# Side work in steps twice as large, one every 1.8 dense units, with groups of prompt attention in turn and selected rows staged in DRAM

## The chip, the cores and the metric

One Trainium2 chip, one of its cores. The metric is device time of one execution in microseconds (us); lower is better. The core has TensorE (PE, with its weight loads as a row of their own, PEld), VectorE (DVE), ScalarE (ACT), GpSimd (POOL) and SyncE (SP). Here SP does nothing but issue DMAs, one after the other, and it stops at each whose semaphores have not come yet.

## The reference, cut to what matters

One layer of a hybrid decoder, for 512 prompt tokens and 8 samples of 4 new tokens each (544 columns together):

```
h = rmsnorm(x); z = h @ w_in                        # 2048 x 14376
A = sparse attention(q, k, v, gates) * silu(.)      # compressed + selected + window
B = causal pooling, group map * silu(.)
C = conv, chunked state-space scan (SSD), silu gate, rmsnorm
y = x + w_out(sum_b sigmoid(G_b) * (m_b @ w_branch_b))
```

For a sample, attention reads a paged cache, `cache_kv` (16 pages of 128 positions, found through `page_table`; a row holds k_cmp, v_cmp, k_slc and v_slc for 2 heads, 256 numbers each), and a window of 512 rows. With 33 blocks the top 16 are selected by a mask, so that the selected branch reads all rows of its pages too.

## The kernel before, in words

**Dense units.** The projections are cut into 612 `Unit`s in one fixed list: `w_in` (kv, gd, q: 84 units; nz, mz: 64; mg first half: 96; pool and xbc: 112; mg second half: 96), then `w_branch`, then `w_out`. A unit is 24 matmuls of 128x128 weights by 272 columns in fp32r: 4 slices of k, three products each (`hhi*wh`, `hlo*wh`, `hhi*wl`), two column halves, summed in a PSUM tile `zin`. Its weights come as `wr` (512 KB for two units, four buffers, L423), are issued six units ahead, and are split three units ahead by ACT (`wh`, L173) and DVE (`wl`, L176).

**Side work.** All the rest (norms, rope, attention, pooling, convolution, SSD) is written as generators. `run_units` calls `step` between dense units, and each step runs every generator in `s.sides` up to its next `yield`. `s.rate` is the number of steps per unit: 1.0, 1.5 in the first half of mg, 1.7 in the second. The order in the program is then changed by a scheduler at build time: each engine gets one fixed order, in which side instructions may stand inside a unit.

**Pools.** `U` gives one of 32 SBUF buffers of 128x608, `A` one of four PSUM banks for side work (`zin` has its own).

**Sample attention** (`samp`): for two pairs of samples, `samp_cmp` makes the compressed keys (`keys4` turns four blocks of `kr` rows through PE into `kT`; then the scores `cS` with weights of only 32 columns) and the compressed values (`pv`, `xvT`, `ocT`); then `samp_group` runs four times over window and selected rows (`kT`, scores `sS`, turned probabilities `sP`, values `sO`). `need` loads row sets two ahead of their use.

**Where the rows come from.** `stage_pages` copies the k_cmp and v_cmp half of every page to a DRAM scratch `ckd`, 128 DMAs, one per step. `rows` reads these sets from `ckd`, four DMAs of 256 KB each. Selected rows come straight from the cache instead: eight DMAs of 128 KB for one set, and for each SP must first load the page number into a register (`page`, L350):

```
if kind > 1:
    nc.sync.dma_start(u[:, o:o + 256], s.page(t, 4 * bl + e)[:, 256 * kind:256 * kind + 256])
```

**Prompt attention** (`attn_p`): for each of two groups of four heads, eight blocks a head: `sa` (scores and exp), `sb` (turn to `PT`), `sc` (values into `O`), one block a step. Both groups run as soon as their q is ready, so that they are interleaved.

Of the kernel before, what the change touches and what calls it, by code (L numbers as in the profile page):

```python
# [19 lines left out]
NP = 512  # L20
# [9 lines left out]
RATE_SSD = 1.7  # L30
RATE_MG = 1.5
# [92 lines left out]
class Prog:  # L124
    def __init__(s, ctx, tc, a):
        s.ctx, s.tc, s.nc = ctx, tc, tc.nc
        s.a = a
        s.n = 0
        s.sides = []
# [223 lines left out]
    def stage_pages(s):  # L353

        nx = s.ids(0, 1, 0, 16)
        for b in range(8):
            t, nx = nx, s.ids(b + 1, 1, 0, 16) if b < 7 else None
            for i in range(16):
                s.nc.sync.dma_start(s.ckd[b][i], s.page(t, i)[:, :512])
                yield  # L360

    def rows(s, raw, q, bl, kind, lq, t):

        nc = s.nc
        b = 2 * q + bl
        for e in range(4):
            if e % 2 == 0:
                u = s.U("kr")
                if kind < 2:
                    src = s.ckd[b].rearrange("i (c l) x -> (i c) l x", l=16)  # L370
                    nc.sync.dma_start(u[:, :512].rearrange("p (l x) -> p l x", l=2),
                                      src[:, 4 * lq + e:4 * lq + e + 2, 256 * kind:256 * kind + 256])
            o = 256 * (e % 2)
            if kind > 1:
                nc.sync.dma_start(u[:, o:o + 256], s.page(t, 4 * bl + e)[:, 256 * kind:256 * kind + 256])
            raw[bl, e] = (u, o)
# [20 lines left out]
    def run_units(s, units, ld=6, lp=3):  # L397
        n = len(units)
        acc = 0.0
        for i in range(n):  # L400
# [4 lines left out]
            if i >= 0:  # L405
                units[i].mm()
                acc += s.rate
# [57 lines left out]
    def norm_rope(s, raws, acc, gains, todo):  # L465
# [5 lines left out]
        for n, u in raws:  # L471
# [14 lines left out]
            yield  # L486

    def stage_kv(s):
# [4 lines left out]
        s.kv_done = False  # L493
        s.ksT = s.dp.tile([128, 2, 2, 32], F, name="ksT")
# [88 lines left out]
    def kv_side(s, kacc):  # L583
# [16 lines left out]
        for i in range(5):  # L600
            r0, rows = (i * 128, 128) if i < 4 else (NP, 32)
            for kind in range(3):
# [12 lines left out]
                yield  # L615
# [65 lines left out]
    def q_side(s, g, qacc):  # L681
# [8 lines left out]
        yield from s.norm_rope(raws, qacc.pop(g), {e: s.gain[:, 0:1] for e in range(4)}, todo)  # L690


    def attn_p(s, g):
        nc = s.nc
        while not s.kv_done:
# [37 lines left out]
        for e in range(4):  # L733
            h = g * 4 + e
            O = s.A("O")
            s.mm(O[:, :NP], s.vc4[32 * e:32 * e + 32, g], pc[32 * e:32 * e + 32, :NP], True, False,
                 skip_group_check=True)
            us = [(br, i) for i in range(4) for br in range(2)]
            PP, PT = {}, {}

            def sa(n):
                br, i = us[n]
                L = i * 128 + 128
                S = s.A("S")
                s.mm(S[:, :L], q[e][:, i * 128:L], s.kv[4 + 4 * br + g][:, :L], True, False)
                s.mm(S[:, L - 128:L], s.identb, s.trib, False, True)
                mx, sm = s.small(1), s.small(1)
                nc.vector.tensor_reduce(mx, S[:, :L], axis=AX.X, op=OP.max)
                s.ts(mx, mx, -1e29, OP.max, -SC, OP.mult)
                P = s.U("P")  # L750
                s.act(P[:, :L], S[:, :L], AF.Exp, bias=mx, scale=SC, accum_out=sm)
                s.ts(sm, sm, 1e-30, OP.max)
                nc.vector.reciprocal(sm, sm)
                c = h * 3 + 1 + br
                s.ts(P[:, :L], P[:, :L], sm, OP.mult, s.gn[:, i, c:c + 1], OP.mult)
                PP[n] = P

            def sb(n):
                br, i = us[n]
                P = PP.pop(n)  # L760
                L = i * 128 + 128
                t = s.A("PT")
                for kt in range(i + 1):
                    s.tr(t[:, kt * 128:kt * 128 + 128], P[:, kt * 128:kt * 128 + 128])
                PT[n] = s.U("PT")
                if n % 2:
                    s.act(PT[n][:, :L], t[:, :L])
                else:
                    nc.vector.tensor_copy(PT[n][:, :L], t[:, :L])

            def sc(n):
                br, i = us[n]
                pt = PT.pop(n)
                for kt in range(i + 1):
                    s.mm(O[:, i * 128:i * 128 + 128], s.Vn[kt][:, br * 256 + g * 128:br * 256 + g * 128 + 128],
                         pt[:, kt * 128:kt * 128 + 128], False, br == 1 and kt == i, skip_group_check=True)
            for n in range(10):
                if n < 8:
                    sa(n)
                if 1 <= n < 9:  # L780
                    sb(n - 1)
                if n >= 2:
                    sc(n - 2)
                yield
            o = s.U("Os")
            s.act(o[:, :NP], O)
            nc.sync.dma_start(s.oT[h][:, :NP], o[:, :NP])
# [3 lines left out]
        for br in range(2):  # L791
            del s.kv[4 + 4 * br + g]

# [17 lines left out]
    def pool_units(s):  # L811
# [11 lines left out]
        def u_side(t, u):  # L823
# [24 lines left out]
            for e in range(gi + 1):  # L848
# [8 lines left out]
                yield  # L857
# [124 lines left out]
    def dt_side(s):  # L982
# [12 lines left out]
        x, e, q, d = s.dtx, s.U("e"), s.U("sq"), s.U("sd")  # L995
        x, e, q, d = (v[:16, :T] for v in (x, e, q, d))
# [71 lines left out]
    def ssd(s):  # L1068
# [5 lines left out]
        for c in range(4):  # L1074
            cs = slice(c * 128, c * 128 + 128)
            xd, yo = [], []
            for g in range(2):
# [6 lines left out]
                yield  # L1084
# [8 lines left out]
            yield  # L1093
            if c:
                for g in range(2):
                    p = s.A("yo")
                    s.mm(p, CT[g][:, cs], St[g][:, :NP])
                    u = s.U("yo")
                    s.tt(s.h64(u[:, :NP]), s.h64(p), s.hb(s.eac[:, c, g * 8:g * 8 + 8]))
                    yo.append(u)  # L1100
                    yield
# [34 lines left out]
            for k in range(6):  # L1136
                if k < 4:
                    ld(k)
                if 1 <= k < 5:
                    dec(k - 1)  # L1140
                if k >= 2:
                    out(k - 2)
                yield
            for g in range(2):
# [8 lines left out]
                yield  # L1153
        osp = a["o_ssm_p"].rearrange("o b h p n -> (o b h p) n")
        for g in range(2):
# [7 lines left out]
            yield  # L1163
        yield from s.ssd_sample(BT, CT, one)
        yield from s.m_norm()
        yield from s.br_early()

    def ssd_sample(s, BT, CT, one):
# [5 lines left out]
        for g in range(2):  # L1174
# [8 lines left out]
            yield  # L1183
# [23 lines left out]
        for b in range(8):  # L1207
            load(b + 2)
            bm = s.dp.tile([32, 256], F, name=s.nm("bm"), tag="bm", bufs=2)
            s.ts(bm, nb[:32, :256], s.c("smask")[:32, b:b + 1])  # L1210
            sT = []
            for g in range(2):
# [9 lines left out]
                yield  # L1222
            for q in range(4):
                o = b * 64 + (q // 2) * 32
                s.mm(py[32 * q:32 * q + 32, :256], cz[:, o:o + 32], sT[q // 2][:, (q % 2) * 256:(q % 2) * 256 + 256],
                     b == 0, b == 7, skip_group_check=True)
            for g in range(2):
# [9 lines left out]
                yield  # L1237
# [30 lines left out]
    def m_norm(s):  # L1268
# [3 lines left out]
        for g in range(2):  # L1272
            P = [s.A("ms") for _ in range(2)]
            for e in range(4):
# [5 lines left out]
                yield  # L1280
                for hf in range(2):
                    s.mm(P[hf][:, :H], s.c("ones"), z[:, hf * H:hf * H + H], e == 0, e == 3)
            ss, rs, tmp = s.U("mss"), s.U("mrs"), s.U("mt")
# [12 lines left out]
    def samp(s):  # L1296
# [11 lines left out]
        ready, pts = [], []  # L1308

        def need(n=1):  # L1310
            while todo and len(ready) < AHEAD + n:
                q, kind, lq = todo.pop(0)
                raw = {}
                t = pts.pop(0) if pts else None
                if todo and todo[0][1] > 1:
                    pts.append(s.ids(2 * todo[0][0], 2, 4 * todo[0][2], 4))
                for bl in range(2):
                    s.rows(raw, q, bl, kind, lq, t)
# [34 lines left out]
    def keys4(s, raw, CI, out):  # L1353

        for ci, bl, g in CI:
# [10 lines left out]
            if ci % 2:  # L1366
                yield


    def samp_cmp(s, x, imp, CI, need):  # L1370
# [8 lines left out]
        for j in range(4):  # L1379
            wt = []  # L1380
            for h in range(2):
                w = W.pop(4 * h + j)
# [11 lines left out]
            yield  # L1394
            for e2 in range(2):
                p = s.A("qw")
                for e in range(2):
                    for h in range(2):
                        o = (e * 2 + h) * 128
                        c = (2 * e2 + e) * 128  # L1400
                        s.mm(p[:, o:o + 128].rearrange("p (b w) -> p b w", b=8), wt[h][:, c:c + 128], qv)
                o = QW[2 * j + e2][:, :NP].rearrange("p (e b h w) -> p e h b w", e=2, b=8, h=2)
                v = p.rearrange("p (e h b w) -> p e h b w", e=2, h=2, b=8)
                for e in range(2):
                    if e2:
                        s.act(o[:, e], v[:, e])
                    else:
                        nc.vector.tensor_copy(o[:, e], v[:, e])
            yield
        for y in range(2):  # L1410
            q = 2 * x + y
            S = s.A("cS")
            for lq in range(4):
                kT = []
# [507 lines left out]
```

## Time and profile before

| | |
|---|---|
| median of 3 runs | 2454.61 us (2452.2 to 2456.29) |
| the profiled execution's own time | 2455.51 us |
| its span in the trace | 2453.7 us |
| PE busy | 2381.8 us, 97% |
| DVE, ACT busy | 1084.9 us, 716.9 us |
| mean granted clock of PE | 0.991 |

The span is the time from the first to the last instruction; 1.8 us of the execution lie outside it. Matmuls overlap in the pipeline, so 97% is the share of time in which at least one is under way; it doesn't say that PE runs at its peak.

### The profile page before, as it was taken

To read this page: it belongs to the slowest core of one execution; us is meant where nothing else is said; L and a number is where in the kernel's file an instruction comes from. 1 tells how busy PE (TensorE), PEld (TensorE's weight loads), DVE (VectorE), ACT (ScalarE), POOL (GpSimd) and SP (SyncE) were. 2 spreads that over 40 slices of the span, in tenths; PEclk is the share of its full clock that TensorE was granted. 3 is DMA by queue.
4 is the path that set the end of the run, shared out by engine and by line. 5 is a ranking of instruction groups with operands and counts; after the bars stand their busy time and mean duration, and the time that the engine had idled before them with its cause. 6 is when DMAs were issued, how large, how long until landed. Compare 5 with 4: busy or idle time off the path is not lost. (4 is left out here: it accounts for less than half of the span.)

```text
span 2453.7 us, 49120 instructions
## 1 busy us (share of the span) xinstructions
PE 2381.8 (97%) x19749; PEld 2239.6 (91%) x19749; DVE 1084.9 (44%) x2206; ACT 716.9 (29%) x1369; POOL 55.7 (2%) x153
## 2 busy tenths in 40 slices
PE   4999999999999999999899999999999999999999
PEld 4999888888998998988798999989999999999999
DVE  5227547555332232423353545555446344445222
ACT  4222333333332222322232233322223322223221
POOL 0001011000000000000000000000000000000000
PEclk9999899999999999999999999999999999999999
DMA  7855563422568567665656543333646664443442
GB/s 213 243 160 147 168 173 99 136 69 75 154 202 246 159 192 227 174 196 162 208 160 196 143 126 89 102 105 111 183 128 196 183 189 132 133 133 99 127 132 81
DMA packets 525668, 377.27 MB, mean 154 GB/s; under 512 B 26895, under 2 KB 472615, under 8 KB 525440
## 3 DMA queue, kind: packets, MB, share of 16 engines
q1 hardware_dynamic: 518528, 360.76, 51.5%
q10 hardware_dynamic: 6912, 13.37, 1.5%
q8 instruction: 155, 2.54, 0.4%
q14 instruction: 73, 0.60, 0.1%
HBM read 328.31 MB, written 79.66 MB: 166 GB/s over the span
## 5 line engine op out<-in xcount | busy, mean ns | idle before, releaser
L153 PE MATMUL zin<-hhi,wh 128*128 128x272 f32 (+1 forms) x3616 | 784.6, 297 | 5.6 <-ACT wh L173 4.6
L176 DVE TENSOR_TENSOR wl<-wr,wh 128x512 fp32r<-128x512 f32 (+1 forms) x612 | 422.9, 693 | 776.4 <-ACT wh L173 772.9
L153 PE MATMUL zin<-hlo,wh 128*128 128x272 f32 (+1 forms) x3616 | 757.7, 290 | 0.0
L153 PE MATMUL zin<-hhi,wl 128*128 128x272 f32 (+1 forms) x3616 | 756.5, 290 | 0.2 <-DVE wl L176 0.2
L173 ACT ACTIVATE wh<-wr 128x512 fp32r<-128x512 f32 (+1 forms) x612 | 382.9, 628 | 1108.7 <-PE zin L153 919.5
L153 PEld LDWEIGHTS zin<-hhi,wh 128*128 128x128 f32 (+1 forms) x3616 | 568.3, 189 | 38.6 <-issue 28.3
L153 PEld LDWEIGHTS zin<-hhi,wl 128*128 128x128 f32 (+1 forms) x3616 | 570.2, 189 | 4.5 <-issue 3.0
L153 PEld LDWEIGHTS zin<-hlo,wh 128*128 128x128 f32 (+1 forms) x3616 | 567.8, 189 | 6.1 <-issue 5.2
L153 PE MATMUL zin<-bh,wh 128*128 128x272 f32 x1280 | 266.4, 290 | 1.1 <-DVE gt L185 1.1
L153 PE MATMUL zin<-bl,wh 128*128 128x272 f32 x1280 | 264.7, 288 | 0.0
L153 PE MATMUL zin<-bh,wl 128*128 128x272 f32 x1280 | 264.4, 288 | 0.0
L153 PEld LDWEIGHTS zin<-bh,wh 128*128 128x128 f32 x1280 | 200.0, 188 | 1.4 <-ACT wh L173 1.3
L153 PEld LDWEIGHTS zin<-bl,wh 128*128 128x128 f32 x1280 | 201.3, 189 | 0.0
L153 PEld LDWEIGHTS zin<-bh,wl 128*128 128x128 f32 x1280 | 201.1, 188 | 0.0
L1364 DVE COPY kT<-kT 128x512 f32<-128x512 f32 x72 | 49.0, 688 | 63.7 <-PE kT L156 63.1
L156 PE MATMUL kT<-cst,kr 128*128 128x128 f32 x512 | 68.9, 276 | 0.0
L156 PEld LDWEIGHTS kT<-cst,kr 128*128 128x128 f32 x512 | 56.6, 141 | 7.7 <-issue 5.7
L173 ACT ACTIVATE mg<-zin 128x544 f32<-128x544 f32 x48 | 29.8, 620 | 101.9 <-PE zin L153 101.9
L173 ACT ACTIVATE P<-S,sm 128x512 f32<-128x512 f32 (+3 forms) x64 | 33.8, 528 | 86.6 <-DVE sm L182 84.3
L173 ACT ACTIVATE kT<-kT 128x512 f32<-128x512 f32 x72 | 42.5, 595 | 33.8 <-PE kT L156 33.2
L153 PE MATMUL S<-kv,q 128*128 128x128 f32 (+3 forms) x128 | 47.1, 452 | 0.2
L153 PE MATMUL O<-PT,Vn 128*128 128x128 f32 x320 | 44.4, 277 | 0.0
(409 smaller groups left out, 1839.4 us busy)
## 6 DMA issues: line engine op xcount, KB each, us to landing
wr<-in_w_in_dram SPq DMA_DIRECT2D x224, 512.0 KB
ckd<-in_cache_kv_dram SPq DMA_DIRECT2D x128, 256.0 KB
kr<-ckd SPq DMA_DIRECT2D x128, 256.0 KB
kr<-in_cache_kv_dram SPq DMA_DIRECT2D x256, 128.0 KB
wr<-in_w_branch_dram SPq DMA_DIRECT2D x48, 512.0 KB
wr<-in_w_out_dram SPq DMA_DIRECT2D x32, 512.0 KB
mgd<-mg ACTq DMA_DIRECT2D x48, 272.0 KB
gt<-mgd SPq DMA_DIRECT2D x48, 272.0 KB
```

The costliest lines, as they stand in the source:

```text
L153: return s.nc.tensor.matmul(out, l, r, start=start, stop=stop, **kw)
L156: return s.nc.tensor.transpose(out, in_, s.c("ident")[:k, :k])
L173: return s.nc.scalar.activation(out, in_, f, **kw)
L176: return (eng or s.nc.vector).tensor_tensor(out, a, b, op=op)
L1364: s.nc.vector.tensor_copy(u[:, :NP], p)
```

## The change

Each generator's step is made about twice as large and its stages are put one step apart, so that what a step uses on PE was made in the step before: in `samp_cmp` and `samp_group`, `scores` of set n-1 stands ahead of `keys4` of set n in one step; values take two sets a step; the probabilities of the compressed branch become a generator of their own. In return there is a step only every 1.8 units (`RATE = 0.55`, and `0.75` in the second half of mg). `attn_p` of group 1 waits until group 0 is through (`s.turn`) and does two blocks of each stage a step. `stage_pages` copies both halves of each page, 256 DMAs, and is driven once per unit by a new list `s.feeds`, whatever the rate is. Selected rows are then read from `ckd` like the others, four DMAs of 256 KB a set with addresses known at build time.

```
-RATE_SSD = 1.7
-RATE_MG = 1.5
+RATE = 0.55
+RATE_SSD = 0.75
...
-        s.rate = 1.0
+        s.rate = RATE
...
-        s.ckd = [dt(f"ckd{b}", [16, 128, 512]) for b in range(8)]
+        s.ckd = [[dt(f"ckd{k}{b}", [16, 128, 512]) for b in range(8)] for k in range(2)]
...
+        for k in range(2):
+            for b in range(8):
+                t, nx = nx, s.ids((b + 1) % 8, 1, 0, 16)
+                for i in range(16):
+                    s.nc.sync.dma_start(s.ckd[k][b][i], s.page(t, i)[:, 512 * k:512 * k + 512])
+                    yield
...
+        k, o = divmod(kind, 2)
+        src = s.ckd[k][b]
+        for e in (0, 2):
+            u = s.U("kr")
+            if k:
+                v = src[4 * lq + e:4 * lq + e + 2].rearrange("i t x -> t i x")
...
+            s.nc.sync.dma_start(u[:, :512].rearrange("p (l x) -> p l x", l=2), v[:, :, 256 * o:256 * o + 256])
+            raw[bl, e], raw[bl, e + 1] = (u, 0), (u, 256)
...
                 units[i].mm()
+                s.feeds = [g for g in s.feeds if next(g, s) is not s]
                 acc += s.rate
...
-        while not s.kv_done:
+        while not s.kv_done or s.turn != g:
             yield
...
+        for n in range(0, 36, 2):
+            for f, d in ((sc, 4), (sb, 2), (sa, 0)):
+                for m in (n - d, n - d + 1):
+                    if 0 <= m < 32:
+                        f(m)
             yield
...
+        for n in range(9):
+            if n:
+                scores(n - 1, kT)
+                kT = None
+            if n < 8:
+                kT = s.keys4(need(), CI)
+            yield
...
-            if j + 2 < 8:
-                W[j + 2] = s.cmp_w(1, j + 2)
+            if j + 3 < 8:
+                W[j + 3] = s.cmp_w(1, j + 3)
...
+        for n in range(0, 6, 2):
+            if n == 2:
+                po = begin(0, nt)
+            if n:
+                for m in (n - 2, n - 1):
+                    sums(po, P.pop(m), need(), 0, m == 3)
+            if n < 4:
+                for m in (n, n + 1):
+                    P[m] = turn(S[m], m)
...
-        s.sides.append(s.stage_pages())
+        s.feeds.append(s.stage_pages())
...
-        units.append(Mark(lambda: s.pace(RATE_MG)))
         units += s.mg_units(0, MGA)
-        units.append(Mark(lambda: s.pace(1.0)))
```

Two places in the built order show what moves. The first is SP's queue in the selected phase of the second sample group. Before, this is the end of a run of selected rows (`pt` is a page table row, `TENSOR_LOAD` and `ISA` set registers), up to the next weight load:

```order
L345 DMA pt_13795<-in_page_table_dram 1x2x4
L350 TENSOR_LOAD pt_13658
L350 ISA x2
L375 ISA
L375 DMA kr_13797<-in_cache_kv_dram 128x256
...
L350 TENSOR_LOAD pt_13658
L350 ISA x2
L375 ISA
L375 DMA kr_13860<-in_cache_kv_dram 128x256
L423 DMA wr_13888<-in_w_in_dram 128x8x128
```

Now, a set of selected rows stands between two weight loads (`no` are small outputs of the pooling branch):

```order
L423 DMA wr_16819<-in_w_in_dram 128x8x128
L374 DMA kr_16571<-ckd_89 128x2x256
L374 DMA kr_16573<-ckd_89 128x2x256
L374 DMA kr_16575<-ckd_90 128x2x256
L374 DMA kr_16577<-ckd_90 128x2x256
L846 DMA out_dram<-no_16614 15x128
L847 DMA out_dram<-no_16614 8x4x128
L423 DMA wr_16898<-in_w_in_dram 128x8x128
```

The register loads are gone from this stretch, a set is four DMAs in place of eight, and fewer of them stand between two weight loads. In the whole program SP has 384 register loads from memory before and 256 now, 1,295 DMAs before and 1,272 now; 71 of the 256 staging copies stand behind the first load of staged rows, none of 128 before.

The second place is PE in the compressed keys of the first pair, with `cS` the scores with narrow weights and `kT` the turned keys. Before:

```order
L153 MATMUL zin_8414<-hlo,wh_8410 128x272 x2
L156 MATMUL kT_8578<-cst,kr_8119 128x128 x2
...
L156 MATMUL kT_8585<-cst,kr_8121 128x128 x2
L153 MATMUL cS_8521<-kT_8535,QW_8103 32x128
L153 MATMUL cS_8521<-kT_8542,QW_8103 32x128
L156 MATMUL kT_8620<-cst,kr_8123 128x128 x2
L153 MATMUL cS_8521<-kT_8583,QW_8103 32x128
L156 MATMUL kT_8620<-cst,kr_8125 128x128 x2
L156 MATMUL kT_8627<-cst,kr_8123 128x128
L153 MATMUL cS_8521<-kT_8590,QW_8103 32x128
```

Now the 16 scores of one set stand together, and behind them the 16 transposes of the next:

```order
L153 MATMUL zin_9937<-hlo,wh_9762 128x272 x2
L153 MATMUL cS_9974<-kT_9867,QW_9342 32x128
L153 MATMUL cS_9974<-kT_9874,QW_9342 32x128
...
L153 MATMUL cS_9974<-kT_9888,QW_9343 32x128
L156 MATMUL kT_9999<-cst,kr_9362 128x128 x2
L156 MATMUL kT_9999<-cst,kr_9364 128x128 x2
...
L156 MATMUL kT_10020<-cst,kr_9368 128x128 x2
L153 MATMUL zin_9937<-hhi,wh_9802 128x272 x2
```

The scores are no longer broken up by transposes. PE's instructions are the same 18,036 matmuls in both programs. The stretches of side work between dense matmuls fall from 425 to 285. Of stretches with 32-column weights that PE enters from 128-column work, those of `cS`, `sS`, `sO` and `nT` fall from 72 to 40. The last `O` comes 164 units into the list, before 136; the last `soT` (the end of sample attention) 333, before 315; the last `ms` (the end of the SSD branch) 403, before 417.

## Rows read from the trace of the kernel before

**Rows 1.** Busy time by stretch (from:to, length, busy; PEclk granted; DMA share, GB/s).
```profile
core 0: us, PE busy (x) PEld busy (x) DVE busy (x) ACT busy (x) POOL busy (x), PEclk, DMA share, GB/s
0.00:45.00 45.00, 13.63 (x61) 11.20 (x62) 26.32 (x74) 22.35 (x59) 0.98 (x6) 0.92 0.71 207
...
200.00:350.00 150.00, 146.46 (x1380) 131.81 (x1378) 94.29 (x161) 44.66 (x82) 18.51 (x22) 0.95 0.58 165
...
620.00:985.00 365.00, 360.18 (x3364) 336.12 (x3363) 113.66 (x212) 102.63 (x189) 1.03 (x12) 1.00 0.68 198
985.00:1430.00 445.00, 421.16 (x3677) 386.24 (x3676) 180.46 (x376) 131.50 (x271) 15.92 (x52) 0.98 0.61 176
```
**Rows 2.** The chain, in order of time: a long dense stretch (start, us).
```profile
1969.98 292.13 PE zin L153 x2328
```
**Rows 3.** Waits, 985 to 1430: us in total, times, longest.
```profile
ACT wh L173 <- DMA wr<-in_w_in_dram: 73.1, 16, 12.8
...
PE sS L153 <- ACT kT L173: 5.8, 2, 5.1
...
PE zin L153 <- ACT wh L173: 4.6, 1, 4.6
```
**Rows 4.** Timeline of SP, 1044 to 1099: start, us, instruction, count.
```profile
1046.39 1.02 SPq L423 DMA_DIRECT2D wr<-in_w_in_dram  x2
...
1055.44 8.48 SPq L375 DMA_DIRECT2D kr<-in_cache_kv_dram  x8
...
1090.20 0.43 SPq L423 DMA_DIRECT2D wr<-in_w_in_dram  x1
```
**Rows 5.** Waits, 1086 to 1098.
```profile
ACT wh L173 <- DMA wr<-in_w_in_dram: 6.0, 1, 6.0
...
PE sS L153 <- ACT kT L173: 5.1, 1, 5.1
```
**Rows 6.** Waits, 959 to 970.
```profile
PE ocT L153 <- DMA cw<-in_cmp_w_dram: 4.2, 2, 3.4
```
**Rows 7.** Waits of PE, 200 to 350.
```profile
PE dn L156 <- DVE dtx L185: 1.8, 1, 1.8
```
**Rows 8.** Busy time by stretch, columns as in rows 1, just behind that wait.
```profile
256.50:270.20 13.70, 13.70 (x89) 10.89 (x89) 3.77 (x16) 3.45 (x10) 0.00 (x0) 0.50 0.13 46
```
**Rows 9.** Timeline of PE, 739 to 742.5.
```profile
739.28 0.42 PE L153 MATMUL zin<-hlo,wh 128*128 128x272 f32 x2
739.54 1.04 PE L156 MATMUL kT<-cst,kr 128*128 128x128 f32 x8
740.51 0.41 PE L153 MATMUL cS<-kT,QW 128*32 128x128 f32 x4
740.85 0.52 PE L153 MATMUL zin<-hhi,wh 128*128 128x272 f32 x2
741.30 0.41 PE L153 MATMUL cS<-kT,QW 128*32 128x128 f32 x2
```
**Rows 10.** Timeline of PE, 680.5 to 685.3.
```profile
683.50 1.06 PE L153 MATMUL cS<-kT,QW 128*32 128x128 f32 x26
684.49 0.55 PE L156 MATMUL kT<-cst,kr 128*128 128x128 f32 x3
684.80 0.50 PE L153 MATMUL zin<-hhi,wh 128*128 128x272 f32 x2
685.13 0.41 PE L153 MATMUL zin<-hhi,wl 128*128 128x272 f32 x2
```
**Rows 11.** Busy time by stretch, columns as in rows 1: compressed values, first pair.
```profile
745.00:795.00 50.00, 49.96 (x460) 44.06 (x459) 14.54 (x28) 13.76 (x25) 0.00 (x0) 1.00 0.94 276
```
**Rows 12.** Timeline of SP, 100 to 112: staging.
```profile
106.57 5.63 SPq L359 DMA_DIRECT2D ckd<-in_cache_kv_dram  x5
```
**Rows 13.** Timeline of SP, 655 to 690: rows from the scratch.
```profile
674.32 3.31 SPq L371 DMA_DIRECT2D kr<-ckd  x6
```
**Rows 14.** Groups of instructions: xcount, busy us, mean ns of one, idle time before.
```profile
L1364 DVE COPY kT<-kT 128x512 f32<-128x512 f32 x72 | 49.0, 688 | 63.7 <-PE kT L156 63.1 <-DMA kr<-ckd 0.2
```

More of the change, by code (lines that the diff above doesn't have):

```diff
@@ L732, in attn_p @@
         yield
[L733 to L787, printed above, removed]
@@ new lines, in sb, with sc @@
+        def sb(n):
+            i = us[n][2]
+            P = PP.pop(n)
+            L = i * 128 + 128
+            t = s.A("PT")
+            for kt in range(i + 1):
+                s.tr(t[:, kt * 128:kt * 128 + 128], P[:, kt * 128:kt * 128 + 128])
+            PT[n] = s.U("PT")
+            if n % 2:
+                s.act(PT[n][:, :L], t[:, :L])
+            else:
+                nc.vector.tensor_copy(PT[n][:, :L], t[:, :L])
+        def sc(n):
+            e, br, i = us[n]
+            pt = PT.pop(n)
+            if n % 8 == 0:
+                OO[e] = s.A("O")
+                s.mm(OO[e][:, :NP], s.vc4[32 * e:32 * e + 32, g], pc[32 * e:32 * e + 32, :NP], True, False,
+                     skip_group_check=True)
+            for kt in range(i + 1):
+                s.mm(OO[e][:, i * 128:i * 128 + 128], s.Vn[kt][:, br * 256 + g * 128:br * 256 + g * 128 + 128],
+                     pt[:, kt * 128:kt * 128 + 128], False, br == 1 and kt == i, skip_group_check=True)
+            if n % 8 == 7:
+                o = s.U("Os")
+                s.act(o[:, :NP], OO.pop(e))
+                nc.sync.dma_start(s.oT[g * 4 + e][:, :NP], o[:, :NP])
@@ L792, in attn_p @@
             del s.kv[4 + 4 * br + g]
+        s.turn = g + 1
     def silu2(s, ps):
@@ L1135, in out @@
                           OP.mult, OP.add)
[L1136 to L1143, printed above, removed]
+            for k in range(4):
+                ld(k)
+            yield
+            if c:
+                for g in range(2):
+                    p = s.A("yo")
+                    s.mm(p, CT[g][:, cs], St[g][:, :NP])
+                    u = s.U("yo")
+                    s.tt(s.h64(u[:, :NP]), s.h64(p), s.hb(s.eac[:, c, g * 8:g * 8 + 8]))
+                    yo.append(u)
+            dec(0)
+            dec(1)
+            yield
+            out(0)
+            out(1)
+            dec(2)
+            dec(3)
+            yield
+            out(2)
+            out(3)
             for g in range(2):
@@ L1206, in ssd_sample, with turn @@
         load(1)
[L1207 to L1210, printed above, removed]
+        def turn(b):
             sT = []
@@ L1221, in ssd_sample @@
                 sT.append(u)
-                yield
+            return sT
+        sT = turn(0)
+        yield
+        for b in range(8):
+            bm = s.dp.tile([32, 256], F, name=s.nm("bm"), tag="bm", bufs=2)
+            s.ts(bm, nb[:32, :256], s.c("smask")[:32, b:b + 1])
             for q in range(4):
@@ L1313, in need @@
                 raw = {}
-                t = pts.pop(0) if pts else None
-                if todo and todo[0][1] > 1:
-                    pts.append(s.ids(2 * todo[0][0], 2, 4 * todo[0][2], 4))
                 for bl in range(2):
-                    s.rows(raw, q, bl, kind, lq, t)
+                    s.rows(raw, q, bl, kind, lq)
                 ready.append(raw)
@@ L1577, in soft, with turn, news @@
             s.tt(sm[:, 7:8], sm[:, 7:8], s.gns[:, q, 1 + br:2 + br])
-            yield sm[:, 7:8]
-        def values(S, br, raws, scale):
-            po = s.A("sO")
-            s.mm(po[:, :128], s.zb[:, :128], s.zb[:, :128], True, False, skip_group_check=True)
+            return sm[:, 7:8]
+        def turn(u, n):
+            p = s.A("sP")
+            for e in range(4):
+                s.tr(p[:, e * 128:e * 128 + 128], u[:, e * 128:e * 128 + 128])
+            pt = s.U("sP")
+            if n % 2:
+                s.act(pt[:, :NP], p)
+            else:
+                nc.vector.tensor_copy(pt[:, :NP], p)
+            return pt
+        def news(br):
             p = s.A("nT")
@@ L1608, in values, with begin @@
-            if br:
-                s.ts(oc[:, q], po[:, :128], scale)
-            else:
-                s.stt(oc[:, q], po[:, :128], scale, oc[:, q], OP.mult, OP.add)
-        mx = s.small(8)
-        got = []
-        yield from keyT(wn, got)
+            return nt
+        def begin(br, nt):
+            po = s.A("sO")
+            s.mm(po[:, :128], s.zb[:, :128], s.zb[:, :128], True, False, skip_group_check=True)
+            s.mm(po[:, :128], nt[:16, :128], vn[:16, br * 128:br * 128 + 128], False, False, skip_group_check=True)
+            return po
@@ new lines, in sums @@
+        def sums(po, pt, raw, o, last):
+            for e in range(4):
+                for ci, bl, g in CI:
+                    v, c = raw[bl, e]
+                    c += o + g * 128
+                    s.mm(po[32 * ci:32 * ci + 32, :128], pt[:, e * 128 + 32 * ci:e * 128 + 32 * ci + 32],
+                         v[:, c:c + 128], False, last and e == 3, skip_group_check=True)
+        kT = s.keys4(wn, CI)
+        yield
+        p = s.A("vn")
+        for br in range(2):
+            s.tr(p[:16, br * 128:br * 128 + 128], vx[:, br])
@@ L1617, in samp_group @@
+        s.act(vn[:16, :256], p[:16, :256])
+        p = scores(kT)
+        mw = s.small(8)
         sw = s.U("sW")
-        s.act(sw[:, :NP], got[0])
+        s.act(sw[:, :NP], p)
         s.tt(sw[:, :4], sw[:, :4], s.c("wneg"), OP.add)
-        nc.vector.tensor_reduce(mx[:, 0:1], sw[:, :NP], axis=AX.X, op=OP.max)
-        for sc in soft([sw], 1, mx, 2):
-            yield
-        yield from values([sw], 1, lambda n: {k_: (u, 256) for k_, (u, _) in wn.items()}, sc)
-        p = s.A("bq")
-        r = slice(32 * q, 32 * q + 16)
@@ L1639, in samp_group @@
             S.append(u)
-            yield
-        for sc in soft(S, 0, mx, 5):
-            yield
-        def raws(n):
+            kT = None
+            if lq == 0:
+                nt = news(1)
+                pw = turn(sw, 0)
+                sw = None
+            if lq == 1:
+                po = begin(1, nt)
+                sums(po, pw, wn, 256, True)
+                s.ts(oc[:, q], po[:, :128], cw)
+                wn = pw = None
+            if lq < 3:
+                kT = s.keys4(need(), CI)
+                yield
+        cs = soft(S, 0, mx, 5)
+        yield
+        nt = news(0)
+        P = {}
+        for n in range(0, 6, 2):
[7 more added lines that the diff above has]
+                    P[m] = turn(S[m], m)
+                    S[m] = None
             if n == 2 and q < 3:
                 s.window(q + 1)
-            return need()
-        yield from values(S, 0, raws, sc)
+            if n < 4:
+                yield
+        s.stt(oc[:, q], po[:, :128], cs, oc[:, q], OP.mult, OP.add)
+        yield
         p = s.A("soT")
@@ L1693, in open_e @@
     def open_e(s):
-        while s.sides:
+        while s.sides or s.feeds:
+            s.feeds = [g for g in s.feeds if next(g, s) is not s]
             s.step()
```

272 lines of the change are left out of this document (136 added, 136 removed).

## The prediction, made blind

> **What bounds the kernel now.** I read the busy time by stretch first. PE is busy almost without a break, so the kernel is PE's queue, and time can come only from three places: what PE's instructions take, PE's idle time, and time at the lower clock. The long dense stretch [rows 2] gives the price of a dense matmul: 292.13 us / 2,328 = 125.5 ns. All 14,688 (612 units of 24) make 1,843 us, or 3.01 us a unit, which no part of the change touches. The other 610 us are side matmuls, the start and the waits. [Rows 1] say where PE idles: 31.4 us in the first 45 us (inputs landing and the norm of x; not touched), 3.5 us from 200 to 350, 4.8 us from 620 to 985, and 23.8 us from 985 to 1430, where the selected rows are read.
>
> Next, the waits of that last stretch [rows 3]: ACT waits 73.1 us for weights `wr`, 16 times. ACT works in its fixed order, so while it waits for a weight it cannot empty the PSUM bank that PE needs next: `sS` waits 5.8 us for `kT` from ACT, `zin` 4.6 us for `wh`. One of these close up [rows 5]: ACT 6.0 us behind a weight, PE 5.1 us behind ACT. Why the weight is late stands in SP's timeline [rows 4]: two weight loads were issued up to 1047.4, the next one at 1090.2. In the 43 us between them SP was issuing four sets of selected rows with their register loads, and a window; eight of these DMAs take 8.48 us to issue. Two weight loads feed four units, 12 us of dense work and some side work, and the six units of lead are used up.
>
> **The change part by part.** I count from the profiled execution's own 2455.5 us (0.9 above the median).
>
> *Selected rows from the scratch.* A set costs SP eight DMAs, 8.5 us, before [rows 4]; four DMAs at 3.31/6 = 0.55 us [rows 13], 2.2 us, after. The same bytes land in SBUF. For 32 sets SP is freed of some 200 us in this stretch. In the built order most weight loads now have one or two sets between them, at worst some 12 us of issuing. So the weights come in time, ACT is not held up, and PE's 23.8 us shrink. The bounds are 0 (something else delays the weights, first rival) and 23.8; I take 20, since bursts of two sets and a window remain. The clock of the stretch is 0.98 of full, so (1 - 0.98) x 445 = 9 us are lost to it, partly inside the idle time; I take 3, of 0 to 9. Sum -23.
>
> Here a rule of the Trainium skill speaks against the change ("DMA: Bandwidth & Descriptors", section "Issuing engines are not separate DMA queues"): the time that a sequencer takes to initiate a DMA is usually small relative to the DMA itself. By it this term would be nothing, and the time that of the first rival. The rows differ from it: 8 x 128 KB at the 276 GB/s of [rows 11] are 3.8 us of transfer, and their issue took 8.48 us [rows 4].
>
> *Weights of the compressed values.* `ocT` waits 4.2 us for `cw` [rows 6], which stood behind selected rows in SP's queue. It is now loaded three ahead; bounds 0 and 4.2, I take -3.
>
> *Longer distance between steps.* `dn` waits 1.8 us for the chain of DVE instructions ahead of it [rows 7]; behind that PE runs at half clock (0.50, the 1.2 GHz level) for 13.7 us [rows 8], which costs up to 6.9 us. With 1.8 units between steps DVE has 5.4 us and more for a step's chain instead of 3. Bounds 0 and 8.7; whether the clock falls I can't tell, so -4.
>
> *Fewer stretches of side work.* 425 become 285. What one costs depends on its matmuls. Dense to transposes costs nothing: a pair of dense matmuls takes its 0.26 us, and eight transposes 0.97 us [rows 9]. From transposes back to dense: three take 0.31 and the next dense pair 0.33 instead of 0.25 [rows 10], about 0.06. Scores with 32-column weights are dear: 26 in a row take 0.99 us, 0.038 each [rows 10], but four between a set of transposes and a dense pair take 0.34 instead of 0.15, and the dense pair behind them 0.45 instead of 0.25 [rows 9]: 0.39 us for one entry. By the built order 32 such entries go (72 to 40): 32 x 0.39 = 12.5. The other 108 stretches at 0.06 are 6.5. Sum -19; bounds 140 x 0.06 = 8 and, if all were as dear, 55, which I don't believe as most of the rest is transposes and full-width matmuls.
>
> *Staging both halves.* 128 copies more, at 5.63/5 = 1.13 us of SP each [rows 12], one a unit. SP can bear this (3.01 us a unit). But 71 of the 256 now run beside the compressed branch, whose value pass already moved 276 GB/s at a share of 0.94 [rows 11], without holding PE up (49.96 us busy of 50). That makes the engines' full rate 276 / 0.94 = 294 GB/s. After, three weight loads in SP's order stand with eight `kr` each: 24 x 0.262 + 3 x 0.524 = 7.9 MB for six units, 18 us dense and by my estimate 8 us side work; 7.9 MB at 294 GB/s need 27 us. So it is at the limit, where before the same sets had a third more units. Bounds 0 and 10 us a pass; I take 4.5, twice: +9.
>
> *At nothing.* Groups of prompt attention in turn and later: covered as long as all side work ends before the branch units; the last `soT` comes at unit 333 and the SSD branch ends at 403 of 452, earlier than before, and the same 12 tiles of `br_early` stand ahead of the end of mg in ACT's order. If that cover went, tiles of about 0.7 us each would be late at unit 452. Splitting probabilities off: same instructions.
>
> Sum: -23 - 3 - 4 - 19 + 9 = -40, 2455.5 - 40 = 2415.5, and at the median 2415.
>
> **The rivals.**
>
> *The DMA engines are what delays the weights.* Then freeing SP gains nothing, and more bytes are moved. For it: the late loads stand in a stretch with much traffic. Against it: [rows 1] show 176 GB/s at 0.61 from 985 to 1430, less than from 620 to 985 (198 at 0.68), where PE idles 4.8 us, most of it the `cw` above. The first term and `cw` fall away: 2455.5 - 4 - 19 + 9 = 2441.
>
> *Slower: staging starves the compressed branch.* From the first turned weight `wT` to the last `ocT` it is 70 units before and 90 after. Before, the stretch of 365 us moved 198 GB/s, 72 MB [rows 1]. After, 20 units more are 60 us and 5 MB of weights, and staging brings 71 x 0.262 = 19 MB: 96 MB in 425 us, 226 GB/s. PE waits for all of it if the engines cannot do that. Copies between two places in DRAM could be dearer than loads. The change turns into a loss only if this eats the 49 us that the other terms give: 96 MB in over 474 us, a rate under 203 GB/s. At 200 it is 480 us: 2455.5 - 49 + 55 = 2461. Against it: 276 was reached [rows 11].
>
> *Slower: five banks wanted of four.* A step of the compressed keys holds `cS` over four steps and turns four `kT`; one of prompt attention wants `O`, two `PT` and two `S`. The fifth must wait until DVE has emptied a bank, 0.69 us [rows 14]. In 32 steps of attention and 36 of keys that is 68 x 0.69 = 47 us: 2455.5 - 40 + 47 = 2462. It decides from 0.6 us a step. Against it: the fourth `kT` starts 12 transposes behind the first, 12 x 0.12 = 1.4 us [rows 9], and the first needs 4 x 0.12 + 0.69 = 1.2 us. Before, with both groups at once, up to six were wanted, and little was waited.
>
> *Nothing moves:* gains and new waits cancel, 2455.
>
> **How the numbers follow.** A difference within 0.2% (5 us) can hardly be told from none here. Forecast 0.76, engines 0.11, staging 0.04, banks 0.05, nothing 0.04. So faster 0.87, same 0.04, slower 0.09. Predicted: 2415. Low end: all idle time and 6 us of clock from the first term (-30), -4, -8, -19, and nothing for staging: 2455.5 - 61 = 2394.5, taken as 2395. High end: the first rival, 2442 with rounding. That holds the forecast and most of the first rival, 0.85 by these chances less what the terms' bounds leave out.
>
> **What would show it.** Right: from the first `sS` to the last `sO`, PE's idle time is under 8 us, ACT's wait for `wr` falls from 73 to under 20 us, and SP never leaves 20 us between weight loads. Stretches of `cS` stand whole at 0.04 us a matmul. `ocT` waits under 2 us. The half clock behind `dn` is shorter or gone. In the compressed branch the DMA share is near 0.8 with peaks over 0.9, and PE waits there for `kr` or for weights behind them, some 9 us. Wrong: ACT still waits for `wr` with SP free (engines); PE waits for `kr` in every key step (staging); PE waits for DVE or ACT copies of `kT`, `PT` or `S` of about 0.7 us, step after step (banks).

## The result and the profile after

The changed kernel takes 2413.62 us (median of 5 runs, 2410.02 to 2414.68), beside 2456.16 us for the kernel before (5 runs on the same chip): a ratio of 0.9824, interval 0.9813 to 0.9835, 1.8% less and clear of the noise. The profiled execution took 2413.62 us, with a span of 2411.9.

| | before | after |
|---|---|---|
| time, us (median) | 2456.16 | 2413.62 |
| PE busy, idle in the span, us | 2381.8, 71.9 | 2360.8, 51.1 |
| mean DMA rate, GB/s | 154 | 170 |

First the busy time by stretch, as [rows 1]. The stages stand later now: the compressed branch at 735 to 1127, the selected phase (first `sS` to last `sO`) at 1155 to 1461, where it was 997 to 1446.

```profile
0.00:45.00 45.00, 12.03 (x55) 9.88 (x55) 23.68 (x66) 22.27 (x58) 0.97 (x6) 0.92 0.68 203
45.00:200.00 155.00, 151.69 (x1183) 147.62 (x1184) 43.57 (x77) 40.01 (x68) 1.26 (x7) 0.98 0.67 192
200.00:350.00 150.00, 144.87 (x1361) 130.76 (x1360) 92.95 (x151) 41.77 (x76) 21.21 (x25) 0.94 0.57 165
...
740.00:1080.00 340.00, 337.30 (x3194) 318.77 (x3193) 102.23 (x187) 96.76 (x177) 1.03 (x12) 1.00 0.79 239
...
860.00:900.00 40.00, 39.22 (x351) 34.02 (x350) 10.79 (x16) 11.07 (x19) 0.00 (x0) 1.00 1.02 309
...
1150.00:1461.00 311.00, 310.37 (x2967) 283.87 (x2966) 167.19 (x361) 111.92 (x234) 19.64 (x61) 1.00 0.69 211
```

PE idles 0.6 us in the selected phase (before, in 985 to 1446, 23.9). The granted clock there is 1.00. But 3.3 us of idle time are new between 45 and 200 (a wait of the start that reaches beyond 45), and from 200 to 350 PE idles 5.1 us, not 3.5, at a clock of 0.94, not 0.95.

Next the waits of ACT, 1000 to 1430, its longest. The row `wh <- DMA wr` of [rows 3] is gone; ACT waits mostly for PE, as it should. One wait of `wh`, 6.0 us, ends as a load of rows lands; it falls into the widest gap between weight loads, shown below, and PE waits for nothing behind it.

```profile
ACT wh L173 <- PE zin L153: 132.9, 57, 4.3
ACT kT L173 <- PE kT L156: 28.4, 32, 3.0
...
ACT wh L173 <- DMA kr<-ckd: 6.0, 1, 6.0
```

SP's timeline at the widest place between two weight loads in this phase, to set beside [rows 4]:

```profile
1195.48 5.00 SPq L423 DMA_DIRECT2D wr<-in_w_in_dram  x2
1202.81 0.34 SPq L892 DMA_DIRECT2D brd<-th  x1
1203.26 4.76 SPq L374 DMA_DIRECT2D kr<-ckd  x8
1208.12 5.30 SPq L1564 DMA_DIRECT2D wn<-in_cache_win_dram  x8
1213.77 5.58 SPq L374 DMA_DIRECT2D kr<-ckd  x8
1219.75 0.33 SPq L892 DMA_DIRECT2D brd<-th  x1
1220.49 0.37 SPq L423 DMA_DIRECT2D wr<-in_w_in_dram  x1
```

Four sets and a window again, but in 20 us, not 43; eight DMAs, two sets, now take about 5 us.

PE's waits at the two ends of what got worse, the start (0 to 200) and 200 to 350, answering [rows 7], and in the compressed branch (740 to 1080):

```profile
PE xT L156 <- DVE x L185: 21.9, 6, 13.3
...
PE gn L156 <- DVE kv L185: 2.8, 1, 2.8
...
PE pv L153 <- DMA kr<-ckd: 1.5, 3, 0.8
PE wT L156 <- DMA cw<-in_cmp_w_dram: 1.2, 2, 1.0
```

The wait of `dn` is gone; `gn` waits 2.8 us in its place (before 0.7). The half clock (0.50) behind `dn` [rows 8] is gone too, but four stretches have come between 200 and 400 (3.4, 6.8, 6.8 and 3.4 us; two of them):

```profile
232.70:236.10 3.40, 3.40 (x17) 3.40 (x16) 2.50 (x5) 1.66 (x3) 1.70 (x2) 0.50 0.42 135
290.80:297.60 6.80, 6.80 (x57) 5.33 (x56) 2.70 (x12) 3.10 (x9) 0.00 (x0) 0.50 0.32 89
```

### The profile page after: what moved, and what is told of

Read it like the earlier page. It is cut to its first block, busy times and chain, and to the rows that moved or that the text cites. A ratio compares the mean times of both kernels' runs of the same rounds, so it can differ in the third digit from the quotient of the medians.

```text
span 2411.9 us, 48472 instructions
## 1 busy us (share of the span) xinstructions
PE 2360.8 (98%) x19749; PEld 2236.4 (93%) x19749; DVE 1091.2 (45%) x2206; ACT 722.8 (30%) x1369; POOL 61.9 (3%) x153
## 4 chain that ended last, share of the span: by engine, by line
PE 93%; DMA 2%; DVE 2%; SPq 1%; issue 1%; POOL 1%; ACT 0%; DVEq 0%; ACTq 0%; POOLq 0%
PE zin L153 74%; PE kT L156 3%; PE O L153 2%; PE S L153 2%; PE y L153 1%; PE sO L153 1%; PE sS L153 1%; DMA kr<-ckd 1%; PE PT L156 1%; PE cS L153 1%; PE ns L153 1%; PE pv L153 1%; PE ocT L153 1%; PE pm L153 1%; PE qw L153 1%
## 5 line engine op out<-in xcount | busy, mean ns | idle before, releaser
L153 PE MATMUL zin<-hhi,wh 128*128 128x272 f32 (+1 forms) x3616 | 772.2, 294 | 0.0
L185 DVE SCALAR_TENSOR_TENSOR gt<-gt,zin 128x544 f32<-128x544 f32 x32 | 23.1, 721 | 48.0 <-PE zin L153 47.9
L173 ACT ACTIVATE P<-S,sm 128x128 f32<-128x128 f32 (+3 forms) x64 | 33.8, 529 | 35.2 <-DVE sm L182 21.9
```

What stands on the lines that cost most here:

```text
L153: return s.nc.tensor.matmul(out, l, r, start=start, stop=stop, **kw)
L173: return s.nc.scalar.activation(out, in_, f, **kw)
L185: return s.nc.vector.scalar_tensor_tensor(out, a, sc, b, op0=op0, op1=op1)
```

## The experiments

Where a difference in us is given, it is that of two ratios times 2456; each ratio's interval is some 0.13% (3 us) to either side, so that the difference of two runs is known to some 5 us.

**Is it the rows from the scratch, or the rarer steps?** `e2_scratch_only` is the kernel before with `rows`, `need` and `stage_pages` of the changed one; `e1_cache_rows` is the changed kernel with the old `rows` and `need`:

```diff
-        for k in range(2):
+        for k in range(1):
...
+            if kind > 1:
+                nc.sync.dma_start(u[:, o:o + 256], s.page(t, 4 * bl + e)[:, 256 * kind:256 * kind + 256])
```

> The kernel before with one part of the change alone: both halves of the pages are staged and the selected rows come from the scratch. Theory A (SP's issue): the -23 of the prediction and at most +5 for staging, so 2433 to 2438; ACT's wait for `wr` from 985 to the last `sO` falls from 73 us to under 20. Theory C (the DMA engines delay the weights, the prediction's first rival): no gain, and 33 MB more to move: 2456 to 2465, with the wait for `wr` still over 40 us. Theory B (rarer steps did it): 2456, with no wait moved.

Measured: 2422.42 us, ratio 0.9866 (0.9847 to 0.9886), -33 us. From 600 to 1600 ACT waits once for `wr`, 2.4 us, and PE hardly idles (row 985 to 1430):

```profile
985.00:1430.00 445.00, 444.97 (x3977) 411.72 (x3976) 195.11 (x403) 141.98 (x286) 18.34 (x58) 1.00 0.63 187
```

This is 11 us below theory A's range, so its -23 was too small. The larger, rarer steps are worth another 10 us on top of it (ratio 0.9866 to 0.9824).

> The changed kernel, but selected rows are read straight from the cache again (eight DMAs with register loads a set), and only the first half of each page is staged. Theory A (SP's issue of the selected rows made the weights late): 20 to 25 us are lost again, less some 3 for the staging that falls away, so 2430 to 2437; ACT waits over 40 us for `wr` in the selected phase, where the changed kernel has no such wait, and SP leaves over 20 us between two weight loads. Theory B (the gain came from the larger, rarer steps alone): 2409 to 2419, and no wait for `wr` returns.

Measured: 2500.89 us, ratio 1.0189 (1.0171 to 1.0208): 90 us lost, four times what theory A gave, and 46 slower than the kernel before. The window 1150 to 1555 holds the whole phase; the second fence is ACT's wait over the run from 600 to 1600.

```profile
1150.00:1555.00 405.00, 358.72 (x3014) 317.15 (x3017) 168.44 (x365) 107.74 (x236) 23.21 (x64) 0.91 0.54 158
```
```profile
ACT wh L173 <- DMA wr<-in_w_in_dram: 91.2, 18, 10.5
```

So both parts work on one thing. The rarer, larger steps pack the 32 sets into 66 units in the changed kernel; before they had 100. From one page table row to the next a set takes SP 10.4 us (1224.85 to 1235.29 in the second fence on SP's timeline below), so that 32 sets need some 334 us by my estimate; the phase took 449 us before and takes 306 in the changed kernel. In this run it takes 403, and SP is idle, in gaps of over 0.2 us, for 16 of them (before 37 of 449, in the changed kernel 155 of 306): SP becomes the bound. Theory B falls; what A lacked is that the larger steps make the old reading dearer.

**SP, or the DMA engines?** `e5_pool_queue` is `e1_cache_rows` with the reads issued by POOL:

```diff
-                nc.sync.dma_start(u[:, o:o + 256], s.page(t, 4 * bl + e)[...])
+                nc.gpsimd.dma_start(u[:, o:o + 256], s.page(t, 4 * bl + e, nc.gpsimd)[...])
```

> As the kernel with rows straight from the cache, but POOL, which is busy 3% of the time, loads the registers and issues these DMAs in place of SP. Same bytes, same DMAs, SP is free. Theory A (SP's issue): nearly all of the 20 us come back, 2409 to 2418, and ACT waits under 10 us for `wr`. Theory C (the DMA engines, or the many transfers with addresses from registers, are the limit): as with SP's issue, 2430 or more.

Measured: 2455.59 us, ratio 1.0004 (0.9992 to 1.0017). Half came back (45 of 90 us). That is far from theory A's range; it is over theory C's 2430, but not the time with SP's issue. ACT's wait for `wr` is gone, but the issue now blocks POOL's own work, and through it DVE and PE (waits, 1150 to 1500):

```profile
DVE ps L176 <- POOLq L350: 9.0, 1, 9.0
...
PE kT L156 <- DVE oc L181: 6.8, 1, 6.8
PE kT L156 <- DVE sS L176: 4.7, 2, 3.4
```

`e14_fixed_pages` settles it: `e1_cache_rows` with fixed page numbers, which need no registers.

```diff
-                nc.sync.dma_start(u[:, o:o + 256], s.page(t, 4 * bl + e)[...])
+                pg = s.a["cache_kv"][0, 16 * b + 4 * lq + e:16 * b + 4 * lq + e + 1].rearrange(...)
+                nc.sync.dma_start(u[:, o:o + 256], pg[...])
```

> As the kernel with rows straight from the cache (2500.9), but the pages are fixed numbers instead of those of the page table, so SP loads no registers for them; its output for the samples is not the reference's. Same count of DMAs and bytes. A set then costs SP 8 x 0.55 = 4.4 us by my estimate from the rows, in place of 8.5. If SP's issue time decides: at least half of the 87 us that the reading from the cache costs comes back, 2430 to 2457, and ACT's wait for `wr` falls from 91 to under 40 us. If the number of DMAs or the small rows are what costs: 2490 to 2502.

Measured: 2413.79 us, ratio 0.9835 (0.9821 to 0.9848), as the changed kernel and better than either range. ACT's waits from 1000 to 1470 have no row for `wr`. SP's timeline of this run, then of `e1_cache_rows`:

```profile
1199.80 3.96 SPq L377 DMA_DIRECT2D kr<-in_cache_kv_dram  x8
1203.81 0.57 SPq L345 DMA_DIRECT2D pt<-in_page_table_dram  x1
1204.48 3.69 SPq L377 DMA_DIRECT2D kr<-in_cache_kv_dram  x8
```
```profile
1205.47 4.20 SPq L376 DMA_DIRECT2D kr<-in_cache_kv_dram  x8
...
1224.85 0.65 SPq L345 DMA_DIRECT2D pt<-in_page_table_dram  x1
1226.84 8.41 SPq L376 DMA_DIRECT2D kr<-in_cache_kv_dram  x8
1235.29 0.65 SPq L345 DMA_DIRECT2D pt<-in_page_table_dram  x1
1237.28 8.74 SPq L376 DMA_DIRECT2D kr<-in_cache_kv_dram  x8
```

The same eight DMAs of 128 KB take about 4 us, not 8.5 (the medians of the 32 sets are 4.5 and 8.4), and begin 0.1 us behind the issue of a page table row, not 1.3. `e1_cache_rows` has sets that take 4.2 us too, as the one at 1205.47: there the registers had been loaded earlier, and no load stands between the DMAs. So neither an address out of a register nor the count of DMAs was the cost, but the register loads, with the few instructions behind each. That there are four DMAs in place of eight, as the change has it, gains nothing that can be told: `e3_first_half` below, which has four and also stages the first halves alone, is 5 us faster, with as much uncertainty. The DMA engines are ruled out: same bytes, same count. The Trainium skill's rule ("DMA: Bandwidth & Descriptors", section "Issuing engines are not separate DMA queues") is that the time to initiate a DMA is usually small relative to the DMA. Neither row agrees: 4 and 8.5 us of issue stand against the prediction's estimate of 3.8 us of transfer.

**Staging.** `e3_first_half`:

```diff
-        for k in range(2):
+        for k in range(1):
...
-        src = s.ckd[k][b]
+        src = s.ckd[0][b]
```

> The changed kernel without the staging of the second halves (128 copies fewer); the selected rows are read from the scratch of the first halves in their place, with the same DMAs and bytes, so its output for the samples is not the reference's. What it takes less is what the second staging costs. By the prediction's term (+9): 2405. By the trace of the changed kernel, where PE waits only 1.5 us for `kr` and 1.2 us for `cw` in the compressed branch: 1 to 4 us, so 2410 to 2413.

Measured: 2411.16 us, ratio 0.9816 (0.9802 to 0.9830): 2 us, less than can be told apart. The term of +9 is not there.

**The price of an entry into narrow weights.** `e4_broken_scores` and `e6_broken_by_four` break the 16 scores up; in the first a group is the four pages of one column group `ci`, in the second one page for all four:

```diff
-            for e in range(4):
+            for ci, bl, g in CI:
...
-                for ci, bl, g in CI:
+                for e in range(4):
...
+                kT[ci] = None
+                if raw:
+                    new += s.keys4(raw, CI[ci:ci + 1])
```
```diff
             for e in range(4):
...
+                if raw:
+                    new += s.keys4(raw, CI[e:e + 1])
```

> The changed kernel with the 16 scores `cS` of a set broken into four groups of four, each followed by four transposes `kT` of the next set: same instructions, same steps, 42 more entries into matmuls with 32-column weights (16 to 58). By the prediction's price of 0.39 us an entry: +16, so 2430. If an entry costs no more than any other break in side work (0.06): +3, so 2416. If fewer entries gained nothing at all and the gain is in the distance between steps: 2414.

> The changed kernel with the 16 scores `cS` of a set in four groups of four, one matmul for each of the four column groups as before, each group followed by four transposes of the next set. 42 more entries into 32-column weights, and the order of the columns is kept, which the earlier kernel with broken scores changed (there eight records of one column group took 1.06 us, where 32 of all four took 1.08 in the changed kernel). By the prediction's 0.39 us an entry: +16, so 2430. By the gaps in the trace of that earlier kernel (0.09 more at each end of a group): 42 x 0.18, +8, so 2421. If entries cost nothing: 2414.

Measured: 2461.84 us, ratio 1.0028 (1.0017 to 1.0039), and 2426.06 us, ratio 0.9872 (0.9856 to 0.9887): +50 and +12 us on the changed kernel. The first was no clean test. PE in the changed kernel, in `e4_broken_scores` and in `e6_broken_by_four`:

```profile
800.40 1.08 PE L153 MATMUL cS<-kT,QW 128*32 128x128 f32 x32
801.41 1.97 PE L156 MATMUL kT<-cst,kr 128*128 128x128 f32 x16
```
```profile
796.23 1.06 PE L153 MATMUL cS<-kT,QW 128*32 128x128 f32 x8
797.23 0.66 PE L156 MATMUL kT<-cst,kr 128*128 128x128 f32 x4
797.81 1.06 PE L153 MATMUL cS<-kT,QW 128*32 128x128 f32 x8
```
```profile
794.93 0.43 PE L153 MATMUL cS<-kT,QW 128*32 128x128 f32 x8
795.29 0.66 PE L156 MATMUL kT<-cst,kr 128*128 128x128 f32 x4
795.88 0.42 PE L153 MATMUL cS<-kT,QW 128*32 128x128 f32 x8
```

Eight records take 1.06 us if all have one column group, 0.43 if they take the four in turn, and a quarter of 1.08 in the whole block of 32. So the four column groups work side by side, and the order of the matmuls gives that or takes it. By the time of the second an entry costs 12 / 42 = 0.28 us, between the two estimates, and the 12 are known to some 5 us only. PE's busy time, less half of what it spent at half clock, grew by 8.4 us (2348.8 to 2357.2), 0.20 us an entry; the rest of the 12 is mostly the clock's. So the price is 0.2 to 0.3 us, under the prediction's 0.39. The Trainium skill ("TensorEngine Tiling (Array Packing)", section "Key Properties") says that different tiles can run in parallel and that a change of tiling mode drains TensorE. These rows agree with the first; the price of an entry fits the second, but no row shows a drain as such.

**The start.** `e8_late_staging` begins staging six units later; `e10_early_consts` loads the constants first:

```diff
+        for _ in range(6):
+            yield
         nx = s.ids(0, 1, 0, 16)
```
```diff
                 mod, = s.cu("mod32")
+                s.tn = s.cu("trineg", "sneg")
...
-        trineg, sneg = s.cu("trineg", "sneg")
+        trineg, sneg = s.tn
```

> The changed kernel with the staging begun six units later. At the start PE waits 13.3 us for DVE, before 9.4; DVE waits for constants `cu`, whose load SP issued 4.5 us later than before, behind page table rows and two staging copies. If these stand in the way: 3 to 5 us less, 2409 to 2411. If the cause is the rarer steps that issue the constants: no change, 2413 to 2415.

> The changed kernel with the constants that DVE casts at the start loaded ahead of most of x, so that the cast no longer stands as a waiting instruction before DVE's scaling of the last x tile. If that wait holds up PE: its gap of 13.3 us falls under 4 and the 13.7 us at half clock behind it get shorter, 9 to 16 us less, 2398 to 2405. Rival: other loads of the start (parameters, weights) are as late, and PE waits for them instead: 2410 to 2415.

Measured: 2409.13 us, ratio 0.9802 (0.9788 to 0.9816), and 2407.38 us, ratio 0.9800 (0.9786 to 0.9814): -5 and -6. The first is as expected, and PE's longest wait at the start falls from 13.3 to 8.9 us. The second gained less. PE's last tile of x in the changed kernel, then in `e10_early_consts`:

```profile
48.31 3.65 PE L156 MATMUL xT<-cst,x 128*128 128x128 f32 x16 [13.27 <-DVE x L185]
```
```profile
41.08 3.65 PE L156 MATMUL xT<-cst,x 128*128 128x128 f32 x16 [5.66 <-DVE x L185]
```

The gap shrank to 5.7, not under 4, and the 13.7 us at half clock to 6.8; DVE waits for nothing in the gap any more, but works through the norm's chain and `wl` up to 40.2.

**Two tiles a step in the norm of keys and queries.** `e9_rope_single`; `e13_early_rope` has this and the early constants:

```diff
-            if m % 2:
-                yield
+            yield
```

> The changed kernel with one tile a step again in the norm of keys and queries, as before, in place of two. In the changed kernel `gn` waits 2.8 us (before 0.7), until DVE has read a bank of `rb`, and PE then runs 3.4 us at half clock. If the four banks of two tiles are the cause (the prediction's third rival, in another place): the wait falls under 1 us and 2 to 5 us are gained, 2409 to 2412. If it is DVE's order, whatever the banks: the wait stays, and the time is 2413 to 2417.

> The changed kernel with the early constants and one tile a step in the norm of keys and queries. If the two gains add up: 2402 to 2405. If the second brings nothing: as the early constants alone, 2405 to 2409.

Measured: 2400.46 us, ratio 0.9780 (0.9766 to 0.9793), -11 us, and 2392.43 us, ratio 0.9745 (0.9732 to 0.9758), -19: both beyond what was expected; the two gains (11 and 6) add up within the noise. PE and clock, 200 to 400, in the changed kernel and in `e9_rope_single`:

```profile
200.00:400.00 200.00, 194.78 (x1720) 176.22 (x1719) 124.01 (x206) 57.75 (x104) 26.63 (x32) 0.95 0.55 160
```
```profile
200.00:400.00 200.00, 199.78 (x1854) 185.31 (x1852) 129.80 (x220) 63.07 (x113) 30.84 (x37) 1.00 0.61 176
```

PE's 5.2 us of idle time and all 20.4 us at half clock are gone. This execution took 2393.67 us at a mean granted clock of 0.997; the other four took 2400.28 to 2404.34 at 0.993 or 0.994, where the five of the changed kernel have 0.990 to 0.994. So the clock's part is shown for one execution alone. Of the four stretches at half clock in the changed kernel only the first follows a long wait, that of `gn` for a bank. Ahead of the third (321.5) `rb` waits 0.9 us for DVE `q`; ahead of the second (290.8) PE was busy with small matmuls (`pc`, `pe`, `acs`, `acT`, from 285.95) and waited for nothing. Why all are gone with the smaller step is not settled: the edit moves all side work of that stage.

**Groups in turn.** `e11_both_groups`:

```diff
-        while not s.kv_done or s.turn != g:
+        while not s.kv_done:
```

> The changed kernel with the two groups of prompt attention at the same time, not in turn. The prediction priced the turns at nothing: 2411 to 2416. If two groups at once want more banks than there are (two steps of `S`, `PT` and `O` in one): PE waits for DVE or ACT copies of about 0.7 us in many of these steps, 2418 to 2435.

Measured: 2411.07 us, ratio 0.9820 (0.9806 to 0.9833): no difference that can be told. Taking turns is worth nothing, and costs nothing.

## Why the prediction was right, and where its terms were not

2415 was forecast and 2414 measured. The mechanism of the largest term is shown by `e2_scratch_only` and `e14_fixed_pages`, but several terms were off and their errors cancelled, so that the hit within 2 us is in part luck:

| term | forecast | measured | from |
|---|---|---|---|
| selected rows | -23 | -28 | idle 23.9 to 0.6; 13.6 us of half clock gone, PE busy in 10.0 of them, half of these lost |
| weights of the compressed values | -3 | -4 | `ocT` waits for nothing |
| distance between steps | -4 | +4 | 200 to 400: idle 4.3 to 5.2, half clock 13.7 to 20.4 us |
| fewer stretches | -19 | -17 | PE's busy time less half of that at half clock: 2381.8 - 31.6/2 to 2360.8 - 24.0/2 |
| staging | +9 | +2 | `e3_first_half` |
| start | none | +5 | 0 to 200: idle 31.4 to 36.3; `e8_late_staging` |

Where no run is named, the figures are those of one profiled execution of each kernel. The row for 200 to 400 before, to set beside that of the changed kernel above:

```profile
200.00:400.00 200.00, 195.66 (x1729) 174.29 (x1726) 130.66 (x232) 62.02 (x113) 25.01 (x32) 0.97 0.57 162
```

The terms sum to -38. Of the other 4 us of the span, 2 are idle time elsewhere, and 2 are a stretch of 3.4 us at half clock at 1809.5, which the changed kernel lacks.

- **Selected rows.** The mechanism was right and the size too small. The clock's share, taken as 3 of at most 9, was 5. A set was priced at 8.5 us of SP; with its page table row and the first register load it took 10.4. The step from eight DMAs to four was credited with the gain, together with the register loads; these alone are it. Nor is a gap of 20 us between weight loads the point from which it hurts: the changed kernel has one of 20.0 in this phase, `e14_fixed_pages` one of 34.2, and PE waited in neither.
- **Weights `cw`.** Gone as forecast, but not for the reason given: `e2_scratch_only` loads them two ahead as before, and `ocT` does not wait there either. It was SP's queue again.
- **Distance between steps.** The step that failed. `dn` was relieved as forecast, but I looked at the longer time for DVE and not at the twice as many PSUM banks that a step of `norm_rope` wants. `gn` waits for DVE to empty a bank of `rb`, which is the third rival's mechanism in a place that it didn't name; with one tile a step again the whole is 11 us faster.
- **Fewer stretches.** PE's matmuls take 17 us less, near the forecast (14 less than in `e2_scratch_only`, which has the old steps). This is read from traces; no run changes the count of stretches alone. The price of a narrow entry was 0.39 by one place of the trace and is 0.2 to 0.3 by `e6_broken_by_four`: 32 of them are 6 to 9 of the 17, not 12.5. What the rest is made of stays open.
- **Staging.** Too dear. In the compressed branch the rate is 239 GB/s at a share of 0.79, near the 0.8 forecast, with 309 GB/s from 860 to 900; I had taken 294 as the full rate. PE lost 2.7 us there, not 9.
- **The start** was left out: the order of SP's queue ahead of the first units was not looked at. SP issues page table rows and two staging copies ahead of the constants `cu`, DVE waits for these in its fixed order, and PE for DVE.
- **The rivals.** The DMA engines do not delay the weights (`e2_scratch_only`, `e14_fixed_pages`). Staging does not starve the compressed branch. Prompt attention and keys do not wait for a fifth bank; the norm does.

## What to carry to other kernels

A queue's issue time is a resource like an engine's: count what stands between two loads that must be in time, register loads first. Two edits can hang on the same resource: the larger steps alone lose 46 us, the scratch alone gains 33, both together gain 43, so that the same steps are worth -46 or +10; test them apart before crediting either. And when a step is doubled, count the banks that it holds beside the time that it leaves; undoing it in the one place where it wants four, with the constants loaded early, gives the best version, `e13_early_rope`, at 2392.43 us (0.9745 of the kernel before).

## What was not expected of the hardware

- With a register load ahead of each DMA, a set of eight took SP 9.8 us behind its page table row (1225.50 to 1235.25), 1.2 us a DMA. With the registers loaded earlier (4.20 for eight) or with fixed addresses (3.96) it took about 0.5 us a DMA: the load is the cost, not the address from a register.
- Matmuls with 32-column weights in four column groups run side by side only if they come in turn: 0.43 us for eight records, 1.06 if one group has them all.
- The clock fell to 0.50 (the 1.2 GHz level) at 290.8 us behind a stretch of small matmuls in which PE waited for nothing.
